# Low-rank weights scaled on ScalarE, and a priority for the first stream's k and r operands

## The chip, the cores and the metric

The kernel runs on one core of a Trainium2 chip. The core has a matrix engine (TensorE, PE in the profile), a vector engine (VectorE, DVE), an activation engine (ScalarE, ACT), a general engine (GpSimd, POOL) and a queue of DMA issues (SyncE, SPq). Each engine works through its own list of instructions in a fixed order, and semaphores hold an instruction back until what it needs is there. An instruction that waits therefore holds back all that stand behind it on its engine. The metric is the device time of one execution in microseconds (us): the median over several runs.

## The reference

Two streams of 512 tokens with 1024 channels (`x_prompt`, here stream 0, and `x_sample`, stream 1) pass through the same two layers. The change lies in what comes ahead of the scan of layer 0 (RWKV-7 time mixing):

```python
xn = _rms_norm(x, pre_norm_g[i])
xx = 0.5 * (x_prev + x_next) - xn
lerp = lambda j: xn + xx * mu[j]
r = heads(lerp(0) @ w_r)
k = heads(lerp(1) @ w_k)
v = heads(lerp(2) @ w_v)
z = xn @ w_z
for d in range(2):
    xw = lerp(3 + d)
    xa = lerp(5 + d)
    w_log = -softplus(-(w0[d] + tanh(xw @ w1[d]) @ w2[d])) - 0.5
    a = sigmoid(a0[d] + (xa @ a1[d]) @ a2[d])
```

`w1`, `a1` (1024 x 64, two directions each) are the low-rank weights. The kernel does not form `lerp(3)` to `lerp(6)`: it multiplies by `w1` and by `diag(mu) w1`, and shifts and adds the small products afterwards. Layer 1 is a neighbourhood attention with a gate.

## The kernel before

Activations lie with channels on the partitions: a stream is 8 tiles of 128 x 512 (`xn`). All large products are made from pairs of fp32r matmuls. An operand `x` is split into `hi`, a cast on ScalarE, and `lo = x - hi`, a subtraction on VectorE (`halves`, L351 to L355). A weight column of 128 outputs is split the same way into `whi` and `wlo`, in two halves of four channel tiles. One column of a product is 8 channel tiles times 3 matmuls (`hi*hi`, `hi*lo`, `lo*hi`), 24 matmuls into one PSUM bank: L404 to L406 ahead of the scan, L747 to L749 during it.

**The prelude**, some 180 us long, is the part that the change touches. `run` (L1627) issues it in program order, and a scheduler at build time reorders it: it simulates the engines, takes what is ready, and prefers the instruction of the lower priority number. Priorities count up in program order; `tc.high_priority(n)` (L374) lowers them by n. Its parts are:

- `prelude(0)`: load stream 0, split it for z (`xz`, L485 and L486), sum of squares and `rstd` (L411 to L444), `xn` (L504), the low-rank weights (`lora_weights`, L447), `xx` (L511, L512), the low-rank products (L528 to L530), their shift (L539 to L549), `tanh` and split (L551, L570, L571), and lv of stream 0 to DRAM (L560, L561).
- `prelude(1)`: the same for stream 1, which in addition writes lk, lr, lv and lz of its stream to DRAM.
- The 8 z columns of stream 0 (operands `xz`), then its 8 k columns (operands `shifted(0, 1)`). One step of the two preludes is issued after each step of a column.
- The operands of r, `shifted(0, 0)`, which the first group of the scan's stream takes up. `shifted` forms `xr` on VectorE (L578, 3 buffers) and splits it into a pair of `act` tiles (L353, L354). There are 18 `act` buffers, so 9 pairs: an operand of k needs the pair that the last z column has done with, one of r that of the last k column.

`lora_weights` handles two of the four low-rank weights at a time: it loads them into `lr` (128 x 1024, one buffer, 512 KB), scales a copy by the seven-way `mu` into `lm` (one buffer) with 16 instructions of 128 x 64, and splits `lr` and `lm` into eight `lw` tiles each (L465 on ScalarE, L466 on VectorE).

**The end of the prelude.** After the last k column comes the norm of k: the sums of squares go through DRAM (`ss`), a square root on ScalarE (L639, which needs a table load), a maximum and a reciprocal on VectorE (L641, L642), and the result (`rn`) is stored and loaded again, repeated over the partitions (`rb`, L791).

**The scan** (`scan_phase`, L1555) and what follows fill the remaining 1500 us. On PE, DVE and ACT the scan's order is written out by a planner (`weave`, L1523) and kept as it is; it begins with the r columns of stream 0 (L747 to L749) and the preparation of the first pair of heads (`prep`, L767): `kk` from `k` and `rb` (L798), the second low-rank weights (L794, split at L800 and L802) and the products with the hidden values (L816, L817).

Of the kernel before, what the change touches and what calls it, by code (L numbers as in the profile page):

```python
# [12 lines left out]
AF = mybir.ActivationFunctionType  # L13
ALU = mybir.AluOpType
# [199 lines left out]
class Trunk:  # L214
# [7 lines left out]
    POST4 = 0.2  # L222
    LAST = ("pg", "pg", "pm", "pm")
    PG, PT, NK, NPT = 2, 2, 2, 3
    AHEAD, AHEADW, SCAN_A, SCAN_W = 0, 0, 300, 300
    NAB, NX, NR, NY, NSB, NBI = 2, 2, 2, 2, 4, 1
    NAK, NZ = 1, 1
    NRR, NTM = 2, 2
# [192 lines left out]
    def rstd(self, acc):  # L421
        run(self.rstds(acc))
        return acc
# [23 lines left out]
    def lora_weights(self):  # L447

        vt, act = self.nc.vector, self.nc.scalar
        self.wl, self.wm = [], []  # L450
        for q2 in range(2):
            raw = self.t("lr", (P, KT * P), 1, F32, self.lp)
            self.load(raw.rearrange("p (q c) -> p q c", q=2), self.a["lora1"][2 * q2:2 * q2 + 2].rearrange("q p c -> p q c"))
            rv = raw.rearrange("p (q k c) -> p k q c", q=2, k=KT)
            m = self.t("lm", (P, KT * P), 1, F32, self.lp).rearrange("p (k q c) -> p k q c", k=KT, q=2)
            for k in range(KT):
                for q in range(2):
                    vt.tensor_scalar(m[:, k, q], rv[:, k, q], self.vec("mu", 8 * (3 + 2 * q2 + q) + k), None, op0=ALU.mult)
            yield
            for src, dst in ((rv, self.wl), (m, self.wm)):  # L460
                for g in range(2):
                    hi = self.t("lw", (P, 4, 2, 64), 16, F32R, self.lp)
                    lo = self.t("lw", (P, 4, 2, 64), 16, F32R, self.lp)
                    sg = src[:, 4 * g:4 * g + 4]
                    act.copy(hi, sg)  # L465
                    vt.tensor_tensor(lo, sg, hi.bitcast(F32), op=ALU.subtract)  # L466
                    dst.append((hi.rearrange("p k q c -> p k (q c)"), lo.rearrange("p k q c -> p k (q c)")))
                yield
# [1158 lines left out]
    def run(self):  # L1627
        self.todo = [(s, pb) for s in range(2) for pb in range(4)]
        self.made, self.hid, self.shift = set(), {}, {}
        self.did = Counter()  # L1630
        self.xz, self.os = [], [[], []]
        mid, prep, first = ExitStack(), ExitStack(), ExitStack()
        self.banks(mid, pf=1, pm=5 - self.SG - self.ZY, us=1)
        if self.SG:
            self.banks(mid, pg=self.SG)
        self.zs = ExitStack()
        self.banks(self.zs, zy=self.ZY)
        self.gt = "zy"
        self.lp = self.pool(first, "right")
        a = self.prelude(0)  # L1640
        for _ in range(self.FIRST):
            next(a)
        a = both(a, self.prelude(1))
        run(self.columns(0, "z", self.xz), (a, 1))
        run(self.columns(0, "k", self.shifted(0, 1)), (a, 1))
        run(a)
        self.xr = self.shifted(0, 0)
        first.close()
        self.front = self.pool(mid, "right")
        self.pp = self.pool(prep, "right")  # L1650
        self.AHEAD, self.AHEADW = self.SCAN_A, self.SCAN_W
        self.scan_phase(mid)
        self.rest(prep, mid)

    def rest(self, prep, mid):
# [15 lines left out]
        for p in range(self.NPA, NP):  # L1671
            run(self.inproj(0, self.xa, p), (a, self.POST0))
            queue.append(self.heads(0, p))
        run(self.out0(1), (a, self.POST))
        while queue:
            next(a)
# [35 lines left out]
def both(*gs):  # L1712
    for g in gs:
        yield from g
# [110 lines left out]
```

## Time and profile before

| | us |
|---|---|
| median of 3 runs | 1723.08 |
| lowest and highest | 1722.53, 1729.99 |
| the profiled execution | 1721.11 |
| its span | 1719.3 |
| PE busy | 1583.5 (92%) |
| DVE busy | 1246.5 (73%) |
| ACT busy | 982.9 (57%) |

A row of the timeline reads: start, length, engine, line, operation, what is written and read, shape and count; brackets give the idle time before it and what ended it. "x7 4.71" are seven instructions from the first start to the last end. A row of the windows gives, for one stretch, its length, the busy time of each engine with its instructions, the granted clock of PE (1.00 is full) and the load of the DMA engines. A row of the waits gives who waited for whom: us in total, times, longest.

### The profile page before, as it was taken

The numbers are of one execution on the slowest core, as the hardware profiler recorded it, in microseconds if no ns is written. First come the engines' busy times: TensorE is split into PE (matmuls) and PEld (weight loads), VectorE is DVE, ScalarE is ACT, GpSimd is POOL, SyncE is SP. The second block draws the span as 40 slices with busy tenths as digits, with TensorE's granted clock in tenths as the row PEclk, the third lists the DMA queues.
The fourth block names the chain that finished last, engine by engine and source line by source line (L and its number), as shares of the span: only waits on it lengthen the run. The fifth ranks groups of instructions, "written<-read, shape, count | busy, mean of one in ns | idle before, by whom it ended". The sixth has DMA issues, their size and how long they took to land. (4 is left out here: it accounts for less than half of the span.)

```text
span 1719.3 us, 45887 instructions
## 1 busy us (share of the span) xinstructions
PE 1583.5 (92%) x18624; PEld 1209.3 (70%) x18624; DVE 1246.5 (73%) x2725; ACT 982.9 (57%) x1975; POOL 24.1 (1%) x94
## 2 busy tenths in 40 slices
PE   7999787999988999789988799999999999999998
PEld 6766555776766767567766677777777787777776
DVE  8986678788877867898788898655565586555474
ACT  5444655767755675656576545544556664555462
POOL 0000000000000000000000000000000000000000
PEclk9989999999999989899999799999999999999999
DMA  5435687786566678766587564547564248555553
GB/s 204 166 117 202 208 278 230 221 273 224 184 201 205 206 239 252 240 217 216 188 263 229 191 209 146 177 147 246 178 197 146 93 147 268 163 164 160 163 169 98
DMA packets 240819, 336.23 MB, mean 196 GB/s; under 512 B 53696, under 2 KB 119360, under 8 KB 240608
## 3 DMA queue, kind: packets, MB, share of 16 engines
q1 hardware_dynamic: 240608, 333.31, 60.4%
q8 instruction: 146, 2.39, 0.6%
q14 instruction: 65, 0.53, 0.1%
HBM read 227.71 MB, written 105.51 MB: 194 GB/s over the span
## 5 line engine op out<-in xcount | busy, mean ns | idle before, releaser
L747 PE MATMUL pm<-act,whi 128*128 128x512 f32 x608 | 272.9, 449 | 13.1 <-ACT whi L699 9.9
L749 PE MATMUL pm<-act,wlo 128*128 128x512 f32 x608 | 248.8, 409 | 18.2 <-DVE wlo L701 18.2
L748 PE MATMUL pm<-act,whi 128*128 128x512 f32 x608 | 248.9, 409 | 7.7 <-DVE act L727 6.1
L404 PE MATMUL pg<-act,whi 128*128 128x512 f32 x448 | 181.4, 406 | 0.0
L405 PE MATMUL pg<-act,whi 128*128 128x512 f32 x448 | 178.1, 398 | 0.0
L406 PE MATMUL pg<-act,wlo 128*128 128x512 f32 x448 | 178.0, 398 | 0.0
L353 ACT CAST whi<-raw 128x512 fp32r<-128x512 f32 x156 | 96.2, 617 | 142.6 <-PE pg L405 71.8
L354 DVE TENSOR_TENSOR wlo<-raw,whi 128x512 fp32r<-128x512 f32 x156 | 106.7, 686 | 73.9 <-ACT whi L353 56.9
L747 PEld LDWEIGHTS pm<-act,whi 128*128 128x128 f32 x608 | 119.3, 196 | 56.3 <-issue 13.9
L749 PEld LDWEIGHTS pm<-act,wlo 128*128 128x128 f32 x608 | 119.9, 197 | 52.1 <-DVE wlo L701 25.4
L748 PEld LDWEIGHTS pm<-act,whi 128*128 128x128 f32 x608 | 120.1, 198 | 30.5 <-DVE act L727 8.6
L701 DVE TENSOR_TENSOR wlo<-raw,whi 128x512 fp32r<-128x512 f32 x152 | 102.8, 683 | 33.3 <-ACT whi L699 32.6
L699 ACT CAST whi<-raw 128x512 fp32r<-128x512 f32 x152 | 92.7, 617 | 27.9 <-PE pm L748 11.1
L404 PEld LDWEIGHTS pg<-act,whi 128*128 128x128 f32 x448 | 84.2, 188 | 23.7 <-issue 8.8
L406 PEld LDWEIGHTS pg<-act,wlo 128*128 128x128 f32 x448 | 84.2, 188 | 18.9 <-issue 2.8
L405 PEld LDWEIGHTS pg<-act,whi 128*128 128x128 f32 x448 | 84.3, 188 | 17.8 <-issue 3.0
L938 DVE TENSOR_TENSOR N<-etmp,N 128x30 f32<-128x30 f32 (+14 forms) x240 | 79.8, 332 | 8.3
L1361 DVE CUSTOM_DVE_ANT_0 sb<-pm,bias 128x256 f32<-128x256 f32 x128 | 50.1, 420 | 47.3 <-PE pm L1353 36.1
L937 DVE TENSOR_TENSOR etmp<-N 128x30 f32<-128x30 f32 (+14 forms) x240 | 78.7, 328 | 4.8
L1364 ACT ACTIVATE sb<-sb,mx 128x256 f32<-128x256 f32 x128 | 64.1, 502 | 30.7 <-DVE mx L1363 30.5
L1022 PE MATMUL pf<-cab 64*64 64x128 f32 (+1 forms) x2048 | 72.4, 270 | 3.4 <-issue 2.4
L1045 DVE TENSOR_TENSOR AK<-zy,cc 128x256 f32<-128x256 f32 x63 | 26.6, 422 | 64.2 <-PE zy L1010 64.0
(363 smaller groups left out, 3379.1 us busy)
## 6 DMA issues: line engine op xcount, KB each, us to landing
dab<-ab SPq DMA_DIRECT2D x32, 1024.0 KB, 7.1
cab<-dab SPq DMA_DIRECT2D x64, 512.0 KB, 4.5
raw<-in_w_in_dram SPq DMA_DIRECT2D x128, 256.0 KB, 2.9
bias<-in_rpb_dram SPq DMA_DIRECT2D x32, 384.0 KB, 4.7
raw<-in_w_z_dram SPq DMA_DIRECT2D x32, 256.0 KB, 4.6
dz<-tmp SPq DMA_DIRECT2D x32, 256.0 KB, 2.2
raw<-in_w_k_dram SPq DMA_DIRECT2D x32, 256.0 KB, 2.5
dk<-tmp SPq DMA_DIRECT2D x32, 256.0 KB, 3.0
```

Of the source, the lines that this page charges most:

```text
L353: self.nc.scalar.copy(hi, src)
L354: (eng or self.nc.vector).tensor_tensor(lo, src, hi.bitcast(F32), op=ALU.subtract)
L404: nc.tensor.matmul(ps, hi, x[k][0], start=(k == 0), stop=False)
L405: nc.tensor.matmul(ps, hi, x[k][1], start=False, stop=False)
L406: nc.tensor.matmul(ps, lo, x[k][0], start=False, stop=(k == KT - 1))
L699: nc.scalar.copy(hi, raw[h])
L701: nc.vector.tensor_tensor(lo, raw.pop(h), hi.bitcast(F32), op=ALU.subtract)
L747: nc.tensor.matmul(ps, hi[:, at], xh, start=(k == 0), stop=False)
L748: nc.tensor.matmul(ps, hi[:, at], xl, start=False, stop=False)
L749: nc.tensor.matmul(ps, lo[:, at], xh, start=False, stop=(k == KT - 1))
L937: vt.tensor_tensor(tv, N[:, q + 1:, q:q + 1].broadcast_to([P, n, q]), N[:, q:q + 1, :q].broadcast_to([P, n, q]), op=ALU.mult)
L938: vt.tensor_tensor(N[:, q + 1:, :q], tv, N[:, q + 1:, :q], op=ALU.add)
```

## The change

Three edits:

```diff
-    AHEAD, AHEADW, SCAN_A, SCAN_W = 0, 0, 300, 300
+    AHEAD, AHEADW, SCAN_A, SCAN_W = 1000, 0, 300, 300
...
             for k in range(KT):
                 for q in range(2):
-                    vt.tensor_scalar(m[:, k, q], rv[:, k, q], self.vec("mu", 8 * (3 + 2 * q2 + q) + k), None, op0=ALU.mult)
+                    act.activation(m[:, k, q], rv[:, k, q], AF.Identity, scale=self.vec("mu", 8 * (3 + 2 * q2 + q) + k))
...
         run(self.columns(0, "k", self.shifted(0, 1)), (a, 1))
+        self.xr = self.shifted(0, 0)
         run(a)
-        self.xr = self.shifted(0, 0)
         first.close()
```

- The 32 multiplications that form `lm` move from VectorE to ScalarE.
- `operands` of `shifted(0, 1)` and `shifted(0, 0)` are issued with a priority of 1000. During the scan `AHEAD` is 300 in both kernels.
- The operands of r are issued ahead of the rest of `prelude(1)` instead of behind it.

Nothing else is added or removed. From the scan's first instructions on, PE, VectorE and ScalarE have the same order in both kernels; on SyncE a few neighbouring DMA issues are exchanged there. In the prelude the orders differ. These are the places on which the prediction rests, read from the two built programs:

- ScalarE, before: the last split of `xz`, `lw`, sum of squares, `whi` of the second z column's second half. After: the last split of `xz`, 16 of L458, that `whi`, `lw`.
- SyncE, before: second `lr`, then one weight load (`raw`). After: that `raw`, then the second `lr`.
- ScalarE, after: `whi`, 6 of L458, the `rstd` copy L444, 10 of L458, the four `lw` casts of the second `lr`, a table load.
- PE: 45 of the low-rank matmuls that stand ahead of the third z column before stand behind or between later columns after. The last four that are left ahead of it read `lw` casts of the second `lr`.
- VectorE: between the evacuation of the sixth z column (L598) and the reciprocal of stream 1 (L435) stand 38 instructions in either kernel, L598 counted.
- ScalarE at the end, before: square root L639, the last `act` cast of r, L722, `whi` of the first r column's second half. After: the last `act` cast of r, four small copies L1568, L722, that `whi`, then L639. SyncE, after: `k` is loaded ahead of the store of `rn`, and the store follows two weight loads.

## The prediction

> **What bounds the kernel now.** I read the page first, then the windows by stage, then the waits of PE in the prelude, then the timelines of single stages.
>
> ```profile
> span 1719.3 us, 45887 instructions
> ```
> ```profile
> 20.00:82.90 62.90, 62.69 (x276) 50.83 (x275) 61.10 (x118) 27.95 (x48) 0.26 (x4) 1.00 0.42 143
> 82.90:98.00 15.10, 9.23 (x31) 6.37 (x29) 15.01 (x29) 7.79 (x12) 0.13 (x2) 0.65 0.13 44
> 98.00:168.00 70.00, 69.96 (x280) 50.59 (x278) 46.77 (x73) 28.64 (x51) 0.13 (x2) 0.98 0.51 180
> ...
> 174.00:179.00 5.00, 0.00 (x0) 0.00 (x0) 4.22 (x9) 3.78 (x8) 0.00 (x0) 0.72 0.64 208
> 179.00:183.00 4.00, 3.89 (x9) 3.00 (x10) 1.74 (x5) 2.18 (x7) 0.00 (x0) 0.50 0.88 204
> ...
> 200.00:1719.00 1519.00, 1410.22 (x17931) 1079.32 (x17929) 1089.27 (x2435) 884.01 (x1806) 18.57 (x46) 0.97 0.62 198
> ```
> ```profile
> PE pm L747 <- ACT whi L699: 8.0, 3, 5.2
> ...
> PE zy L405 <- DVE act L354: 3.6, 3, 2.3
> ...
> PE pm L625 <- ACT tmp L621: 1.9, 1, 1.9
> ```
>
> From 20 us on PE sets the pace: 276 matmuls in 62.9 us without a gap, one each 0.228 us. Two places break that. From 82.9 to 98 VectorE is full (15.01 of 15.10) and PE waits for k operands and for the norm of stream 1; from 174 to 179 PE does nothing and waits for a weight cast on ScalarE. At half clock (0.50) it then loses a little more. Between them, 98 to 168, PE is full again. Behind 200 us all three computing engines keep their order, so what the change can do is to start the scan sooner or later; I take it that the rest moves along, PE being 93% busy there (1410.22 of 1519).
>
> **The scaling moved to ScalarE.** First its price.
>
> ```profile
> 26.39 2.68 DVE L458 TENSOR_SCALAR lm<-lr,cv 128x64 f32<-128x64 f32 x16
> ...
> 14.85 1.34 ACT L485 ACTIVATE act<-xn,cv 128x512 fp32r<-128x512 f32 x2
> ...
> 178.44 1.13 ACT L699 CAST whi<-raw 128x512 fp32r<-128x512 f32 x2
> ...
> 180.25 1.01 ACT L1568 COPY cab<-cc 64x64 f32<-64x64 f32 x4
> ```
>
> Sixteen cost VectorE 2.68 us, so it is relieved of 5.4 us. ScalarE has no 128x64 instruction with a scale from memory. The nearest row, four copies 64 wide in 1.01 us, gives 0.25 us each; two splits of 512 with such a scale take 1.34 us against the 1.13 us of two casts, so a scale may add 0.1 us: 0.35 is the upper bound. I take 0.25: 4.0 us for a block of 16, up to 5.6.
>
> The 5.4 us of VectorE are worth little: between 20 and 75 us its queue holds evacuations of z columns in order (L598), so it waits there for PE whatever it has saved. What counts is ScalarE's queue:
>
> ```profile
> 17.14 0.61 ACT L353 CAST whi<-raw 128x512 fp32r<-128x512 f32 x1
> ...
> 22.64 0.38 SPq L309 DMA_DIRECT2D lr<-in_lora_dram  x1
> ...
> 23.22 0.66 DVE L354 TENSOR_TENSOR wlo<-raw,whi 128x512 fp32r<-128x512 f32 x1
> ...
> 24.40 0.87 DVE L438 TENSOR_SCALAR tmp<-cc,rs 128x128 f32<-128x128 f32 x4
> ...
> 26.14 0.62 ACT L465 CAST lw<-lr 128x512 fp32r<-128x512 f32 x1 [1.82 <-DMA lr<-in_lora_dram]
> ...
> 29.89 0.59 ACT L444 COPY vs<-pm 128x512 f32<-128x512 f32 x1
> ...
> 30.16 0.39 PE L528 MATMUL us<-act,lw 128*128 128x512 f32 x1
> ...
> 32.01 4.71 DVE L504 SCALAR_TENSOR_TENSOR xn<-xn,cv,vs 128x512 f32<-128x512 f32 x7
> ...
> 36.65 0.67 DVE L598 TENSOR_TENSOR tmp<-zy,vs 128x512 f32<-128x512 f32 x1
> ...
> 42.76 0.40 PE L404 MATMUL zy<-act,whi 128*128 128x512 f32 x1
> ```
>
> 1. The first block stands from 16.1 to 20.1 ahead of the weight cast that ran at 17.14, which ends at 20.7. PE arrives there at about 20.9: it loses perhaps 0.2 us, because the five matmuls ahead of it are no longer held up by L458 on VectorE.
> 2. The square root of the norm, behind the block too, ends at 22.9. On VectorE its scaling, the four L438 as in the row at 24.40 (0.8 us) now stand ahead of the weight subtraction that ran at 23.22, which frees a `raw` buffer at 24.8. SyncE can issue that load only then, and the second `lr` behind it: 25.5 instead of 22.64. Its data needed 3.5 us (22.64 to 26.14), so they are there at 29.0.
> 3. ScalarE then does 16 multiplications (4.0 us) with L444 between them (0.6 us): the first `lw` cast of that block ends at 34.2 instead of 26.8, the one of `lm` at 35.3. L444 ends at 31.1 instead of 30.5.
> 4. PE has in its order 15 low-rank matmuls at 27.5 to 31.0, and then the one on that first cast: it waits 3.2 us, does two, waits 0.6 us for the other cast, does two. The third z column needs the bank that L598 empties, and L598 stands behind seven L504 (4.64 us from start to start) that wait for L444: 31.1 + 4.64 + 0.67 = 36.4. It starts at 36.5. In the kernel before it started at 42.76 with 45 more matmuls done, that is at 42.76 - 45 x 0.228 = 32.5 on an equal count. PE is 4.0 us late.
>
> To this comes the clock:
>
> ```profile
> 86.00:90.00 4.00, 3.09 (x11) 2.19 (x11) 4.00 (x7) 1.03 (x2) 0.00 (x0) 0.68 0.18 66
> ...
> 98.00:100.00 2.00, 2.00 (x7) 1.61 (x6) 1.27 (x2) 2.00 (x4) 0.00 (x0) 0.50 0.46 142
> ```
>
> After pauses of 2.3 us and less (the row of L405 in the waits) at 83 to 88 the granted clock fell, and stayed at half until work had run for over 3 us. Such a fall costs at most half of some 3.4 us, 1.7 us, at least nothing. I take 1.0, since the new pauses (3.2, 0.6, 1.2 us) are like those. So PE is 5.0 us late, with bounds 3.5 (data of `lr` sooner, no fall) and 9 (two blocks at 0.35 add 3.2 us).
>
> The Trainium skill, "TensorE: Matmul & The Clock Gate", Part 1, says that the clock is halved after an idle window of about 3.4 us and restored after a busy one. By it three pauses each below 3.4 us need not fall out of full clock, and the total would be 1.0 us less than mine; the rows at 83 to 90 show a fall after shorter pauses with a few matmuls between.
>
> **The priority of the operands and the earlier place of r.** This is to cut the wait from 82.9 to 98.
>
> ```profile
> 69.47 0.69 DVE L598 TENSOR_TENSOR tmp<-zy,vs 128x512 f32<-128x512 f32 x1 [0.35 <-PE zy L406]
> ...
> 93.81 0.17 DVE L435 RECIPROCAL rs<-rs 128x4 f32<-128x4 f32 x1
> ...
> 96.22 2.04 PE L442 MATMUL pm<-tmp,ones 128*128 128x128 f32 x8 [2.26 <-DVE tmp L438]
> ...
> 97.92 0.77 PE L404 MATMUL zy<-act,whi 128*128 128x512 f32 x1
> ```
>
> VectorE is gated by PE at 69.47 and full from there: 38 instructions in 24.3 us, 0.64 each. In the changed program 38 stand in the same stretch: the k operands 2 to 4 come sooner, but the fifth, for which PE waits first, is 27th there instead of 25th, and the norm is not nearer. A priority helps only what is ready, and from the second on an operand of k has to wait for the last z column to give back its buffers. Gain at 97.92: nothing; by two places out of order 1.3 us to either side. So the second k column starts at 103, and since PE is full from 98 to 168, the last k column ends 5.0 us late too. What this priority pushes back, stream 1's preparation, has its cover in that stretch (VectorE 46.77 of 70).
>
> **The end of the prelude,** where the lag is partly made up.
>
> ```profile
> 169.16 0.67 ACT L621 ACTIVATE tmp<-zy,cv 128x512 f32<-128x512 f32 x1
> ...
> 169.88 1.02 PE L625 MATMUL pm<-tmp,cc 128*2 128x512 f32 x2 [1.92 <-ACT tmp L621]
> ...
> 175.38 1.28 ACT L639 ACT_TABLE_LOAD   x1
> ...
> 178.66 0.33 SPq L309 DMA_DIRECT2D drn<-tmp  x1
> ...
> 179.11 0.80 PE L747 MATMUL pm<-act,whi 128*128 128x512 f32 x1 [5.25 <-ACT whi L699]
> ...
> 181.50 1.11 SPq L309 DMA_DIRECT2D rb<-drn  x2
> ...
> 183.28 0.43 SPq L309 DMA_DIRECT2D tmp<-in_lora_dram  x1
> ...
> 189.89 0.62 ACT L800 CAST w2h<-tmp 128x512 fp32r<-128x512 f32 x1
> ...
> 190.56 0.50 PE L816 MATMUL pm<-h,w2h 128*128 128x512 f32 x1 [1.19 <-ACT w2h L800]
> ```
>
> L621 and the L625 behind it come 5.0 us later, at 174.2 and 174.9. VectorE has used that time for its backlog, so the operands of r follow ScalarE closely: five casts, a small copy and a tanh in 0.5 to 0.6 us each, with one turn over VectorE (subtraction 0.6, next `xr` 0.7), bring the last `act` cast to 179.9; the four small copies 1.0, L722 0.5, and the weight cast ends at 182.0. PE goes on at 182 instead of 179.1, after 3 us of pause instead of 5.25 and hence at full clock: column 0 of r ends 1.9 us late, column 1 at about 190.5 (1.3 late).
>
> The square root, which was ahead of that cast, now follows it with its table load: 183.5 instead of 176.9. Reciprocal done at 185.4, store of `rn` at 185.5 (178.66 before), `rb` loaded 2.8 us after it as before, and the second low-rank weights issued at 189.5 (4.6 us after the store before, less 0.6 for the load of `k`, which has moved ahead). The DMA engines are less loaded there than before:
>
> ```profile
> tmp<-in_lora_dram SPq DMA_DIRECT2D x16, 256.0 KB, 5.3
> ```
>
> Such a load took 5.3 us in the median; that of `lr` took 3.5 us from issue to use. I take 3.5: L800 at 193.0 instead of 189.89, and L816, the first matmul of the scan's preparation, 3.1 late. Sum: +3 us, with bounds -3 (no lag, 5 us of pause gone, half of it given to the norm's round trip) and +9. On the profiled execution's 1721.1 us (span 1719.3 and 1.8 around it) that is 1724; the median of the runs lies 2.0 above it, so 1726.
>
> **The rivals.**
> - The scan starts a little sooner (1720). If the second `lr` arrives as early as before, PE has no pause at 31 to 36, and the pause at 174 shrinks by some 3 us because the weight cast no longer follows the square root. For it: 5.25 us are there to win. Against: the load stands behind another that waits for VectorE.
> - The priority does work (1711). If the pauses of 82.9 to 98 go, 15.1 us shrink to the 5 to 6 us that its 31 matmuls need, and 1.6 us of half clock after it go too: -11, or about -5 with the lag of the first part. For it: VectorE's 15.01 of 15.10. Against: 38 instructions in either order.
> - Slower (1733). ScalarE's multiplications cost 0.35 us, the clock falls, PE is 9 us late, and the norm's round trip, now last in line, takes the median 5.3 us for its load: store at 189.4, L800 at 198.7, +9 to +10. It decides from where the store of `rn` is issued after about 187 us. For it: each step is serial on ScalarE from L621 to the square root. Against: the same engine was idle for half of the prelude.
>
> **How the numbers follow.** Forecast (0 to +6) 0.48; sooner 0.16; the priority works 0.10; slower 0.26. About 0.5%, 8.6 us, is what a measurement of this kernel tells from no change. Slower by that: three quarters of the slower rival and a little of the forecast, 0.21. Faster: most of the second rival, 0.08. Within: 0.71. The range 1717 to 1735 takes in the bounds of the unknown prices, at the low end the priority working with the first part's lag (1718), at the high end the slower rival with the 2 us that lie between the profiled execution and the median; the forecast's own is 1722 to 1729.
>
> **What would show it.** Right: sixteen L458 on ScalarE in about 4 us, twice; the second `lr` issued after 25 us; a pause of PE at 31 to 36 us that waits for `lw` of L465 and then for L598; VectorE still full ahead of the second k column, which starts 3 to 6 us later; the L747 pause shorter, the store of `rn` 5 to 8 us later, L816 at about 193. Wrong: no pause at 31 us, or the second k column starting before 97.9; or a scan that is longer or shorter by itself from L816 to the end, which would break the assumption that it moves as a whole.

## The result, and the profile after

| | before | after |
|---|---|---|
| median, 20 runs each | 1724.41 us | 1730.83 us |
| lowest and highest | 1720.69, 1731.70 | 1725.56, 1740.08 |
| profiled execution, its span | 1721.11, 1719.3 | 1728.38, 1726.5 |

The ratio is 1.0035, with a 95% interval of 1.0020 to 1.0049: 3.4 to 8.4 us slower, 6.0 in the middle. The forecast was +3 (its own range reached to +6), the predicted time 1726, the range 1717 to 1735. The effect, +6.0, lies at the edge of the forecast's own range and midway between its +3 and the +9 to +10 of the slower rival. That the time fell into the stated range says little by itself, since that range is 18 us wide and takes in the rivals too.

The windows of the changed kernel by stage (length, busy time of PE, PEld, DVE, ACT and POOL with their instructions, granted clock, DMA share, GB/s):

```profile
31.00:37.00 6.00, 2.17 (x5) 1.00 (x4) 4.92 (x8) 5.98 (x19) 0.00 (x0) 0.83 0.14 45
37.00:43.00 6.00, 5.80 (x16) 4.43 (x16) 6.00 (x11) 2.06 (x3) 0.00 (x0) 0.60 0.00 0
43.00:83.00 40.00, 40.00 (x175) 32.53 (x174) 35.26 (x57) 13.42 (x24) 0.26 (x4) 1.00 0.42 145
83.00:98.00 15.00, 10.91 (x42) 8.41 (x41) 14.94 (x25) 8.87 (x16) 0.13 (x2) 0.83 0.35 105
```

Before, the stretch from 20 to 82.9 us had no gap to speak of in PE's work (62.69 of 62.90 us). Now there is a hole at 31 us, and the clock is down for some time behind it: 16 matmuls in the 6 us from 37 to 43. From there to 83 us PE is full at full clock, as before, so what was lost by 43 us stays lost. The timeline of the changed kernel shows how it comes about:

```profile
16.07 3.92 ACT L458 ACTIVATE lm<-lr,cv 128x64 f32<-128x64 f32 x16
...
24.77 0.68 DVE L466 TENSOR_TENSOR lw<-lr,lw 128x512 fp32r<-128x512 f32 x1
...
25.48 0.38 SPq L309 DMA_DIRECT2D lr<-in_lora_dram  x1
...
30.03 1.55 ACT L458 ACTIVATE lm<-lr,cv 128x64 f32<-128x64 f32 x6 [1.43 <-DMA lr<-in_lora_dram]
...
31.95 2.49 ACT L458 ACTIVATE lm<-lr,cv 128x64 f32<-128x64 f32 x10
34.34 1.12 ACT L465 CAST lw<-lr 128x512 fp32r<-128x512 f32 x2
...
35.00 0.79 PE L528 MATMUL us<-act,lw 128*128 128x512 f32 x1 [3.83 <-ACT lw L465]
...
37.46 0.80 PE L404 MATMUL zy<-act,whi 128*128 128x512 f32 x1 [0.20 <-DVE tmp L598]
...
40.19 0.63 PE L404 MATMUL zy<-act,whi 128*128 128x512 f32 x1
40.61 0.63 PE L405 MATMUL zy<-act,whi 128*128 128x512 f32 x1
...
41.85 0.39 PE L405 MATMUL zy<-act,whi 128*128 128x512 f32 x1
```

The reader is to follow the data of the second `lr`: its load goes out at 25.48 (22.64 before), the data are used at 30.03 (26.14), the multiplications fill ScalarE to 34.34, the casts that PE reads end 8 us later than before, and PE stands for 3.83 us. Then its matmuls come 0.42 us apart (40.19 to 40.61), not 0.228, up to 41.85. The lag can be read off at marks that both kernels have:

| mark | before | after | late |
|---|---|---|---|
| third z column, start on an equal count | 32.5 | 37.46 | 5.0 |
| L442 of stream 1, ahead of the second k column | 96.22 | 104.17 | 8.0 |
| last L625, behind the last k column | 169.88 | 178.06 | 8.2 |
| L747, first r column, behind the pause | 179.11 | 186.10 | 7.0 |
| L816, preparation of the scan | 190.56 | 198.52 | 8.0 |
| end of the span | 1719.3 | 1726.5 | 7.2 |

The end of the changed kernel's prelude, again from its timeline:

```profile
104.17 2.04 PE L442 MATMUL pm<-tmp,ones 128*128 128x128 f32 x8 [2.21 <-DVE tmp L438]
...
178.06 1.02 PE L625 MATMUL pm<-tmp,cc 128*2 128x512 f32 x2 [1.72 <-ACT tmp L621]
...
182.58 0.75 DVE L578 SCALAR_TENSOR_TENSOR xr<-xx,cv,xn 128x512 f32<-128x512 f32 x1
...
183.36 0.62 ACT L353 CAST act<-xr 128x512 fp32r<-128x512 f32 x1 [2.55 <-DVE xr L578]
...
185.44 0.61 ACT L699 CAST whi<-raw 128x512 fp32r<-128x512 f32 x1
...
186.10 0.79 PE L747 MATMUL pm<-act,whi 128*128 128x512 f32 x1 [4.08 <-ACT whi L699]
...
189.34 0.35 SPq L309 DMA_DIRECT2D drn<-tmp  x1
...
197.37 0.59 ACT L612 COPY tmp<-pm 128x512 f32<-128x512 f32 x1 [4.58 <-issue]
197.85 0.62 ACT L800 CAST w2h<-tmp 128x512 fp32r<-128x512 f32 x1
...
198.52 0.51 PE L816 MATMUL pm<-h,w2h 128*128 128x512 f32 x1 [1.24 <-ACT w2h L800]
```

and the windows of the changed kernel there:

```profile
174.00:179.00 5.00, 3.28 (x11) 0.98 (x9) 5.00 (x9) 3.07 (x6) 0.00 (x0) 1.00 0.76 271
...
186.00:192.00 6.00, 5.90 (x14) 4.54 (x15) 2.21 (x5) 2.42 (x5) 0.60 (x2) 0.50 0.80 276
```

The weight cast does stand ahead of the square root now, and the pause before L747 is shorter (4.08 against 5.25 us). But VectorE was full to 182.58 with `xr` of L578, which ScalarE's last `act` cast waits for, and PE then ran 14 matmuls at half clock, where the kernel before ran 9. Between the last L625 (8.2 us late) and L747 (7.0) the shorter pause gives back 1.2 us; five more matmuls with 0.2 us too much each take 1.0 of it again.

### The profile page after: what moved, and what is told of

Read it like the earlier page. It is cut to its first block, busy times and chain, and to the rows that moved or that the text cites. A ratio compares the mean times of both kernels' runs of the same rounds, so it can differ in the third digit from the quotient of the medians.

```text
span 1726.5 us, 45896 instructions
## 1 busy us (share of the span) xinstructions
PE 1592.8 (92%) x18624; PEld 1217.7 (71%) x18624; DVE 1244.2 (72%) x2693; ACT 991.2 (57%) x2007; POOL 24.3 (1%) x94
## 4 chain that ended last, share of the span: by engine, by line
PE 64%; DVE 16%; ACT 8%; DMA 8%; issue 4%; SPq 1%; DVEq 0%; ACTq 0%
PE pg L404 6%; PE pg L405 6%; PE pg L406 6%; PE pm L747 5%; PE pm L749 4%; PE pm L748 4%; PE pm L1353 3%; PE pf L1022 2%; PE us L1119 2%; PE po L1381 2%; PE zy L1093 2%; DVE etmp L937 2%; PE pt L1368 2%; PE us L1133 2%; DVE N L938 2%
## 5 line engine op out<-in xcount | busy, mean ns | idle before, releaser
L747 PE MATMUL pm<-act,whi 128*128 128x512 f32 x608 | 274.9, 452 | 11.1 <-ACT whi L699 8.3
L747 PEld LDWEIGHTS pm<-act,whi 128*128 128x128 f32 x608 | 120.7, 199 | 54.5 <-issue 13.5
```

What stands on the lines that cost most here:

```text
L747: nc.tensor.matmul(ps, hi[:, at], xh, start=(k == 0), stop=False)
```

## The experiments

The third edit moves nothing by itself: with it alone, the built program has the order and the waits of the kernel before on every queue, and without it the program of the other two edits is that of the changed kernel. It was not run by itself. All ratios are to the kernel before, on the same chip.

**E1, the scaling alone.**

```diff
-                    vt.tensor_scalar(m[:, k, q], rv[:, k, q], self.vec(...), None, op0=ALU.mult)
+                    act.activation(m[:, k, q], rv[:, k, q], AF.Identity, scale=self.vec(...))
```

> Only the scaling on ScalarE; no priority, r in its old place. Theory (the scaling is the cause): the pause of PE at 31 to 35 us stands as in the changed kernel, PE is some 8 us late at L442 and at the last L625. In the built program the square root L639 stands ahead of L722 and the L699 cast again, which makes the pause before L747 about 1.5 us longer than in the changed kernel: ratio to the kernel before 1.0035 to 1.005 (1729 to 1732 us). Rival (the priority, by its late store of rn, costs the time): no more than 1.001.

Measured: 1732.26 us, ratio 1.0044 (1.0020 to 1.0068). PE waits 4.09 us at L528, L442 comes at 103.76, L816 at 197.97. The scaling alone gives the whole loss. The pause before L747 is 4.97 us, 0.9 longer than in the changed kernel, yet it ends at the same time, because the last k column was 0.9 us sooner.

**E2, the priority alone.**

```diff
-    AHEAD, AHEADW, SCAN_A, SCAN_W = 0, 0, 300, 300
+    AHEAD, AHEADW, SCAN_A, SCAN_W = 1000, 0, 300, 300
```

> Only the priority of 1000 (in the built program the earlier place of r then moves no instruction, so this stands for the second and third edits together). Theory: a few L578 and L354 stand two or three places earlier on VectorE, the second k column starts within 1.5 us of 97.9, ratio 0.999 to 1.001. Rival (the priority costs the time): 1.002 to 1.004. Rival (the priority works): below 0.997.

Measured: 1724.03 us, ratio 1.0003 (0.9982 to 1.0024); L442 at 96.19, L816 at 189.87. No effect is seen, as the theory had it.

**E6, only the second block on ScalarE.**

```diff
-                    act.activation(m[:, k, q], ...)
+                    act.activation(m[:, k, q], ...) if q2 == 1 else vt.tensor_scalar(m[:, k, q], ...)
```

> The changed kernel with the first 16 multiplications back on VectorE; the second 16 stay on ScalarE. Theory (the first block makes the second lr late): the second lr is issued at about 22.6 us as in the kernel before, its lw cast ends near 30.8, PE waits for it 1 us or less instead of 3.8, third z column 0 to 3 us later than in the kernel before on an equal count, ratio 1.000 to 1.002. Rival (the second block, which stands between the data and the casts, makes the pause): PE waits over 3 us, ratio 1.003 to 1.005.

Measured: 1731.21 us, ratio 1.0042 (1.0018 to 1.0066). Neither expectation held. `lr` is issued at 22.54 and PE has no wait at L528, as the theory said; but L442 is 3.9 us late and L816 4.4. PE and the windows of this kernel:

```profile
37.11 0.50 PE L404 MATMUL zy<-act,whi 128*128 128x512 f32 x1 [1.98 <-DVE tmp L598]
...
31.00:37.00 6.00, 4.13 (x18) 3.00 (x16) 6.00 (x11) 3.33 (x6) 0.00 (x0) 1.00 0.16 44
37.00:43.00 6.00, 5.89 (x19) 4.72 (x20) 6.00 (x11) 1.25 (x2) 0.13 (x2) 0.72 0.00 0
```

The wait has moved from the low-rank matmul to the third z column, which the build had put directly behind the fewer matmuls that were ready: 18 matmuls instead of 28 from 31 to 37, then a fall of the clock (0.72). The ratio lies where the rival had it, but not by the rival's wait.

**E5, only the first block on ScalarE** (the same line with `q2 == 0`).

> The changed kernel with the second 16 multiplications back on VectorE; the first 16 stay on ScalarE. E6 showed that the second block alone makes PE 4 us late at L442. Theory (each block delays by its own way; the first through the second lr, issued at 25.5 us): data at 29.0, casts of lr end at 29.8 to 31.5 with no multiplications ahead of them, PE waits under 1 us at L528, third z column 1 to 3 us late on an equal count, L442 at 98 to 100. Rival (the first block costs nothing, the second does it all): L442 within 0.7 us of 96.2.

Measured: 1730.61 us, ratio 1.0013 (0.9996 to 1.0031); `lr` issued at 25.34, L442 at 100.36, L816 at 196.18:

```profile
32.33 0.50 PE L528 MATMUL pf<-act,lw 128*128 128x512 f32 x1 [0.78 <-ACT lw L465]
33.55 0.50 PE L530 MATMUL us<-act,lw 128*128 128x512 f32 x1 [0.49 <-DVE lw L466]
38.79 0.50 PE L404 MATMUL zy<-act,whi 128*128 128x512 f32 x1 [2.18 <-DVE tmp L598]
...
37.00:43.00 6.00, 4.21 (x18) 3.49 (x19) 6.00 (x11) 1.26 (x2) 0.13 (x2) 1.00 0.00 0
```

At L442 the first block costs 4.1 us (just beyond what was expected), the second 3.9 (E6), both 8.0. That these add up may be chance: each build has its own order. Here the clock stays up (1.00) and the loss is in the waits; VectorE, with the second multiplications to do, is later with L598. L816 is 5.6 us late, but the runs are not clearly slower; 5.6 us would be a ratio of 1.003, at the upper end of the interval.

**E7, the pause filled.** On the line that picks the low-rank weights, 17 matmuls into a bank that the next matmul starts anew:

```diff
-                    a, b = (m[:, k % 4] for m in w[2 * q2 + k // 4])
+                    a, b = (m[:, k % 4] for m in w[2 * q2 + k // 4]); [nc.tensor.matmul(out, self.wm[1][1][:, 0], hi, start=True, stop=True) for _ in range(17 * (s == 0 and k == 0 and q2 == 1 and w is self.wl))]
```

> The changed kernel with 17 additional matmuls (lw of the first block by an act tile, 3.9 us of PE, overwritten by what follows) just ahead of the pause at 31 us. Theory (the pause costs twice: its length, and the half clock of 35 to 42 us after it): the third z column still starts at 37 to 38 us, but at full clock, L442 of stream 1 comes at about 101 instead of 104.2, and the time falls by 2 to 3 us though more is computed: ratio 1.0015 to 1.0025. Rival (the clock falls whatever PE does, or the half clock is made up later anyway): 1.0035 or more.

> E7 once more, since its ratio (0.9987) lies further below the changed kernel's than its prelude explains (L816 3.3 us sooner). Theory (the rest was scatter of the scan): ratio 1.000 to 1.0025, L816 within 0.7 us of 195.3. Rival (the added matmuls help beyond the prelude): ratio below 0.9995 again.

Measured: 1722.10 us, ratio 0.9987 (0.9963 to 1.0011), and the second time 1726.99 us, 0.9989 (0.9969 to 1.0008). Of the first:

```profile
37.45 0.50 PE L404 MATMUL zy<-act,whi 128*128 128x512 f32 x1 [0.68 <-DVE tmp L598]
...
37.00:43.00 6.00, 5.55 (x24) 4.61 (x25) 6.00 (x11) 2.06 (x3) 0.00 (x0) 1.00 0.00 0
...
101.30 2.04 PE L442 MATMUL pm<-tmp,ones 128*128 128x128 f32 x8 [1.06 <-DVE tmp L438]
```

The third z column starts when it did in the changed kernel (37.46), but at full clock: 24 matmuls from 37 to 43 us instead of 16, and eight matmuls are 1.8 us. At the sixth L598, the end of the sixth z column, this kernel is 1.7 us ahead of the changed one (75.32 against 77.05). L442 comes 2.9 us sooner (101.51 the second time: 2.7), but the 1.1 us beyond 1.7 come after that, where the build has put some instructions of VectorE and PE in another order than in the changed kernel. So of the 8.0 us, 5 are the wait and about 2 the half clock behind it; the last 1 is not assigned. L816 comes at 195.26 and 196.61, still 4.7 and 6.1 us later than before. The second set was expected at 1.000 to 1.0025 and L816 within 0.7 us of 195.3; neither came, and a ratio below 0.9995 twice is what the rival had said (the added matmuls help beyond the prelude). The prelude does not explain it, and it stays open (see the last section).

**E8, the casts first.** All 32 multiplications stay on ScalarE, behind the casts of `lr`:

```diff
-            for k in range(KT):
-                for q in range(2):
-                    act.activation(m[:, k, q], ...)
             yield
             for src, dst in ((rv, self.wl), (m, self.wm)):
+                for k in range(KT if src is m else 0):
+                    for q in range(2):
+                        act.activation(m[:, k, q], ...)
```

> The changed kernel with the casts and subtractions of lr issued ahead of the multiplications, all 32 of which stay on ScalarE. Theory (not ScalarE's work costs, but its place between the data of lr and the casts that PE reads): PE has no pause for lw at 31 us and no half clock at 35 to 42, the third z column waits at most 2 us for L444 and what follows it, L442 of stream 1 at 96 to 100, ratio 0.999 to 1.002. Rival (8 us of ScalarE work cost the time wherever they stand): L442 at 104, ratio 1.0035.

Measured: 1725.81 us, ratio 0.9994 (0.9973 to 1.0015); L442 at 98.29, L816 at 193.16. ScalarE's timeline in this kernel (the multiplications are at L460):

```profile
16.50 0.60 ACT L465 CAST lw<-lr 128x512 fp32r<-128x512 f32 x1
17.01 3.22 ACT L460 ACTIVATE lm<-lr,cv 128x64 f32<-128x64 f32 x13
20.13 0.61 ACT L465 CAST lw<-lr 128x512 fp32r<-128x512 f32 x1
...
26.05 0.62 ACT L465 CAST lw<-lr 128x512 fp32r<-128x512 f32 x1
27.04 1.54 ACT L460 ACTIVATE lm<-lr,cv 128x64 f32<-128x64 f32 x6 [0.37 <-DVE lw L466]
28.49 0.61 ACT L465 CAST lw<-lr 128x512 fp32r<-128x512 f32 x1
```

and its window behind the pause of the others:

```profile
37.00:43.00 6.00, 5.56 (x25) 4.25 (x24) 6.00 (x11) 1.26 (x2) 0.13 (x2) 1.00 0.00 0
```

The same 8 us of ScalarE's work cost 2 us at L442 instead of 8, with no wait for `lw` and full clock from 31 to 43 us. Its interval (to 1.0015) lies below that of the changed kernel (from 1.0020). The place decides, not the work.

**E10, VectorE relieved where it is full.** The kernel before, without the change:

```diff
-            self.sumsq(acc, t[:, 1:T + 1], k, vt if s or k % 2 else vt)
+            self.sumsq(acc, t[:, 1:T + 1], k, gps if s else vt)
```

> The kernel before with the seven additions L419 of stream 1 (4.2 us of VectorE from 72 to 89 us) on GpSimd; nothing of the change. Theory (VectorE's queue from 69 to 98 us sets the second k column, and relief counts only there): VectorE reaches L435 and L438 about 4 us sooner, L442 at 91 to 93 instead of 96.2, L816 2 to 4 us sooner, ratio 0.9975 to 0.999. Rival (GpSimd's additions are slow and the norm waits for them, or VectorE is slowed beside them): L442 at 96 or later, ratio 1.000 or more.

> E10 once more, since its ratio (0.9956) lies further below 1 than its prelude explains: L816 came only 0.9 us sooner than in the kernel before, while L442 came 2.4 us sooner. Theory (the scan's own length differs from execution to execution, and part of that gain was scatter): ratio 0.9965 to 0.9995, L816 at 188.5 to 190.5. Rival (the order with the additions on GpSimd shortens the scan itself): ratio below 0.9965 again.

Measured: 1720.35 us, ratio 0.9956 (0.9934 to 0.9979); the second time 1723.87 us, 0.9983 (0.9960 to 1.0006). L442 at 93.83 and 93.34 instead of 96.22, L816 at 189.63 and 188.11 instead of 190.56. L442 comes sooner, as the theory had it, though by less than expected; the first ratio is below its range, the second in it. Of GpSimd (the groups from 60 to 100 us) and of VectorE (timeline) in the first:

```profile
L419 POOL TENSOR_TENSOR acc<-tmp,acc 128x512 f32<-128x512 f32 x7 | 10.9, 1554 | 0.5
...
77.15 1.68 DVE L571 TENSOR_TENSOR h<-lr,h 64x512 fp32r<-64x512 f32 x1
78.86 1.67 DVE L354 TENSOR_TENSOR act<-xr,act 128x512 fp32r<-128x512 f32 x1
80.45 1.78 DVE L605 SCALAR_TENSOR_TENSOR tmp<-tmp,tmp 128x512 f32<-128x512 f32 x1
82.16 1.75 DVE L578 SCALAR_TENSOR_TENSOR xr<-xx,cv,xn 128x512 f32<-128x512 f32 x1
83.83 0.68 DVE L354 TENSOR_TENSOR act<-xr,act 128x512 fp32r<-128x512 f32 x1
...
90.81 0.17 DVE L435 RECIPROCAL rs<-rs 128x4 f32<-128x4 f32 x1
```

L435 comes at 90.81 instead of 93.81. VectorE is rid of 4.8 us of additions, but six of its instructions beside them take 1.06 to 1.78 us instead of 0.68, which is 5 us more: the relief is paid back. What gains is the order: the sum of squares is ready sooner, so that eight more instructions (of the 38 that stood between the sixth L598 and L435, 23 are left) now come behind L435. The length of that queue does set L442, as predicted; the load that was lifted from it is not what shortened it. The gain at L816 is smaller than at L442, since the pause before L747 has grown (6.63 and 6.39 us).

**E12, E8 and E10 together; and the changed kernel again.**

> E8 (all scaling on ScalarE, behind the casts of lr) and E10 (seven L419 of stream 1 on GpSimd) together. Theory (VectorE's relief counts where VectorE is full, from 69 to 98 us, and the 5.4 us that the scaling frees before 40 us count nowhere): no better than E10 alone, since E8 begins 2 us behind: L442 between 93.8 and 97, L816 at 189 to 193, ratio 0.995 to 0.999. Rival (both reliefs add up): L442 below 93, ratio below 0.994.

> The changed kernel once more, beside the same runs of the kernel before as E12. Theory (late lw casts of the second lr and the fall of the clock behind them, no scatter): PE waits 3.5 to 4.2 us at L528, L442 at 104, L816 at 197 to 199, ratio 1.002 to 1.005.

Measured: E12 1723.67 us, ratio 0.9981 (0.9969 to 0.9993), L442 at 95.65, L816 at 190.16: no better than E10. The changed kernel again: 1730.15 us, ratio 1.0042 (1.0023 to 1.0060), with 3.99 us of wait at L528, L442 at 104.87 and L816 at 199.88 (expected up to 199). E10 and E12 beat the changed kernel with intervals that do not meet its own. E12 beats the kernel before too, and E10 did so the first time but not clearly the second.

## Why the prediction was right, and where its sizes were wrong

The direction, the place and the mechanism of the loss came as predicted, but for the reason why the second `lr` comes late (item 2); the size was about half of what came. The forecast made L816 3.1 us late; it was 8.0.

1. **The price of the multiplications.** Taken as 4.0 us for 16; measured 3.92, and 1.55 + 2.49 = 4.04. Right.
2. **The second `lr`.** Issued at 25.48 (predicted 25.5), but for another reason, so that the agreement is luck. The prediction gave the weight load ahead of it on SyncE. The traces show the buffer: `lr` has one, and L466 reads the first `lr` until 25.45 (24.77 + 0.68). In the kernel before, the last reader ends at 22.61 and the load goes out at 22.64; in E8 21.98 and 22.01. The data took 4.5 us (25.48 to 30.03) and not the 3.5 that were taken over from the kernel before: 1 us.
3. **The pause.** Predicted 3.2 us at L528, third z column at 36.5, 4.0 late; measured 3.83, 37.46 and 5.0. The difference is the 1 us of the load.
4. **The clock, a term of the sum that was mis-sized.** It was taken at 1.0 us and bounded at 1.7, half of one stretch of 3.4 us. PE ran at half clock from 35.0 to about 41.8, two such stretches. The four matmuls at 35.0 to 37 cost nothing by it, since the third z column had to wait for L598 behind them anyway (0.20 us). The ten from 37.46 to 41.85 took 4.39 us instead of 2.28: 2.1 us. E7, which takes the pause away, is 1.7 to 1.8 us ahead behind this stage. The bound left out that a fall can last two stretches.
5. **The priority and the earlier place of r.** Predicted to gain nothing; E2 has L442 at 96.19 against 96.22, and the third edit moves no instruction. VectorE was full in that stretch (14.94 of 15 us from 83 to 98 in the changed kernel as well), and E10 shows that fewer instructions ahead of L435 would have helped. That the 5.4 us saved on VectorE bring nothing came true as well, though not by the reason given, that VectorE waits for PE anyway: before, it was busy for 61.10 of the 62.90 us from 20 to 82.9. The saved time turned into waiting (35.26 busy of 40 us from 43 to 83, 38.20 before) while PE stayed full.
6. **The end of the prelude.** Predicted to give back 1.9 us: pause down to 3 us, PE back at full clock, column 1 of r 1.3 us late. It gave back 0.2. The step that failed is "VectorE has used that time for its backlog": it was full (5.00 of 5 us from 174 to 179), with work of stream 1 (L560) still between the operands of r, and its L578 at 182.58 held the last cast. The clock fell here as well, for 14 matmuls instead of 9.
7. **The norm's round trip**, the slower rival. Its condition came true, with the store of `rn` at 189.34 (from 187 on it was to decide), and so did PE's 8 to 9 us. But it did not decide: L800 stands on ScalarE behind L612 of the second r column, which waits for PE and ended only at 197.96. In E1 the store goes out 2.7 us sooner (186.69), and L816 comes only 0.6 us sooner, again directly behind PE's second column. The scan waited for PE's own lag.
8. **The scan moves along.** It did within 1 us in the profiled execution: 8.0 late at L816, 7.2 at the end. That it came so close is partly luck: from L816 to the end the profiled executions of all these kernels took 1522.0 to 1534.1 us. The medians, 6.0 us apart by the ratio, carry the statement.

In sum 1.0 (load) + 1.1 (clock) + 1.7 (end) makes 3.8 of the 4.9 us between the predicted 3.1 and the 8.0 of L816. The other 1.1 us come between 43 us and the last L625 and are not assigned, but for 0.4 in VectorE's 38 instructions ahead of L435, which took 24.7 us (77.05 to 101.75) instead of 24.3. The first rival (sooner) fell at step 2, the second (the priority works) at step 5.

The Trainium skill, "TensorE: Matmul & The Clock Gate", Part 1, calls the watching window free-running, so that the count of slow matmuls differs from run to run of one kernel. The traces agree: E1 has the changed kernel's order through this stage and a pause within 0.3 us of it, and its granted clock from 37 to 43 us is 0.73, where the changed kernel has 0.60 and, the second time, 0.57. The page's idle window of about 3.4 us as the condition of a fall does not fit: in E6 the clock fell behind a pause of 1.98 us.

## What to carry to other kernels

Work that is moved to an idle engine is paid for by what stands behind it in that engine's queue: ask first whether it comes ahead of a cast that the busiest engine waits for, and put it behind (E8: 2 us instead of 8 from the order alone). Relief counts only ahead of an instruction that PE waits for: 5.4 us taken from VectorE before 40 us gained nothing that a run shows, eight instructions put behind L435 gained 2.4 us at L442 (E10). When a pause of PE is priced, add the half clock behind it, and let the upper bound hold two stretches of it (here 6.8 us at half clock, of which 2.1 us were lost).

## What the runs showed of the hardware

**The scan's length differs by several microseconds between executions of one program.** The groups of L833 (first and last start; the first instance stands at the beginning of the scan, the last at its end) for the kernel before, the changed kernel, E7, E7 again and E10:

```profile
L833 DVE TENSOR_TENSOR_SCAN th<-cc,u x16: 1170/1217/1219, 203.0 to 996.3; 128x512 f32<-128x512 f32 x16
```
```profile
L833 DVE TENSOR_TENSOR_SCAN th<-cc,u x16: 1186/1218/1220, 211.8 to 1001.8; 128x512 f32<-128x512 f32 x16
```
```profile
L833 DVE TENSOR_TENSOR_SCAN th<-cc,u x16: 1170/1218/1219, 208.3 to 993.9; 128x512 f32<-128x512 f32 x16
```
```profile
L833 DVE TENSOR_TENSOR_SCAN th<-cc,u x16: 1187/1217/1218, 209.9 to 1000.5; 128x512 f32<-128x512 f32 x16
```
```profile
L833 DVE TENSOR_TENSOR_SCAN th<-cc,u x16: 1171/1217/1219, 203.0 to 989.7; 128x512 f32<-128x512 f32 x16
```

That is 793.3, 790.0, 785.6, 790.6 and 786.7 us with the same order on PE and, but for a few instructions at the beginning, on VectorE and ScalarE; the two of E7 are one program, and E10 again takes 793.0 (200.6 to 993.6). The windows of these stretches for E7, E7 again, E10 and E10 again say where the difference lies:

```profile
208.30:993.90 785.60, 701.59 (x11904) 530.71 (x11894) 637.34 (x1201) 502.48 (x989) 14.78 (x42) 0.94 0.72 227
209.90:1000.50 790.60, 698.11 (x11873) 528.70 (x11872) 637.21 (x1202) 502.59 (x989) 14.81 (x42) 0.94 0.72 225
203.00:989.70 786.70, 700.47 (x11873) 529.84 (x11872) 637.28 (x1201) 502.48 (x988) 14.81 (x42) 0.94 0.72 226
200.60:993.60 793.00, 707.57 (x11872) 536.50 (x11871) 637.47 (x1201) 501.06 (x988) 14.77 (x42) 0.93 0.72 225
```

Between the two of E10, PE's pauses are alike (86.2 and 85.4 us) and PE is busy 7.1 us longer at a lower mean clock, which fits half clock that comes or stays away. Between the two of E7 it is the other way: PE is busy 3.5 us less, but stands for 92.5 us instead of 84.0. So half clock alone does not explain the scatter; what lengthens the pauses is not shown. Marks in the prelude repeat better, at L442 within 0.2 us (E7), 0.5 (E10) and 0.7 (the changed kernel), at L816 within 1.4 to 1.5, and so settle some of what medians of 12 runs leave open. Scatter of single executions does not explain why E7 stayed below 1 in both sets of runs.

**GpSimd beside VectorE.** A 128x512 addition took 1.55 us on GpSimd against 0.68 on VectorE, and four of VectorE's instructions beside it took 1.67 to 1.78 us instead of 0.68. The Trainium skill, "GPSIMD Engine Reference", section 8, says that the two share their interfaces to SBUF and contend where VectorE reads two inputs there; these rows agree, and put a price on it.
